# Index scores, one convolution tile and the threshold search of an encoder layer in another order

## Chip, cores and metric

The kernel runs on 1 core of one Trainium2 chip. The metric is the time of one execution on the device in microseconds. Before the change it is 2482.51 us, the median of 3 runs (2481.71 to 2482.91).

## What is computed

One layer of a streaming encoder on 1088 frames (1024 of a prompt, 64 of a sample with 128 cached positions), 1024 features, float32. Cut to the part around the change:

```python
h = x + 0.5 * swiglu(rms(x), ffn1)
u = rms(h); z = u @ w_in              # q, k, v, q_idx, k_idx, w_idx, conv input, gates
q, k, qi, ki = rope(q), rope(k), rope(qi), rope(ki)
s = relu(qi_head @ ki.T)              # 8 index heads
score = sum_head(wi * s)              # per frame and key, keys up to the frame's chunk
keep = top 256 keys of each frame     # (or a quarter of the keys)
attn = softmax(q @ k.T over keep) @ v
c = ca * sigmoid(cb)                  # 512 channels, depthwise causal conv of width 31
conv_out = silu(layernorm(conv(c))) @ conv_w_out
h = h + (g_a * (attn @ attn_w_out) + g_c * conv_out) @ w_out
h = h + 0.5 * swiglu(rms(h), ffn2); y = rms(h)
```

Besides y it returns the new k, v, index keys and the last 30 rows of c.

## The kernel before

Frames lie along the free axis, features on the 128 partitions. Matrix products run as three float32r matmuls (high by high, low by high, high by low half, mm3, L135 to L137). In the middle of the kernel, between the two feed-forward blocks, TensorE makes the projections of u: `uproj(wt, c)` (L551) is one of three column chunks of 364, 362 and 362 frames, 24 matmuls into one PSUM bank. Weights come by DMA in the order of a packed layout and are split into halves by ScalarE (L117) and GpSimd (L118).

The pieces that the change touches:

- `conv_in(t)` (L604): the two projections of convolution tile t (128 of 512 channels), a tanh on ScalarE (L609), a product on VectorE (L618), and the store to DRAM. `conv(t, dve)` (L646) is the depthwise convolution: for tiles 0, 1 and 2 (dve False) ScalarE makes the 30 shifted products (L675) and GpSimd adds them (L676), in two pieces; for tile 3 (dve True) VectorE does 30 multiply-adds (L661) in each of three pieces, 90 in all, with the sum in a PSUM bank.
- `rope` (L564): six operations on VectorE (L574 to L579) on a pair of chunks in PSUM; `rope_pairs` calls it for the index queries and for the queries.
- Index scores (L768 to L788): for seven tiles of frames (sizes L of 384, 512, 640, 768, 896, 1024 keys, and 192 for the sample's 64 frames; numbered 0 to 6 in the code) and eight heads, a pair of matmuls (L778, L779), relu on ScalarE (L780), and a weighted sum into Y on VectorE (L783, L785). 88 pairs in all.
- The threshold search (L803 to L952) finds for each frame the value of its 256th best score, bit by bit: first the upper 15 bits of the scores as int16, then the lower 16. For each bit, `count` counts how many keys lie above a candidate: tiles 5 and 4 (1024 and 896 wide) on ScalarE (L871, settled by L891 and L892), the other five on VectorE (L874, settled by L880, L882, L884). Ahead of it stand first counts and sign flips (L847 to L859), between high and low bits a transition (L920 to L930: one more count of each tile, L925, and a mask, L928), and behind it the bias for the attention (L934 to L952).
- Attention: `soft` makes logits (L1023, L1024) into three banks, VectorE adds the bias and finds the maximum (L1026); then come transposes (L1050) and values. In the background run two of the 16 gate tiles (L965 to L976; 14 stand before), norm(2) of the convolution's LayerNorm (L1112 to L1139), conv_out (L1157) and the merge.

The order on each engine is fixed at build time: a tile framework simulates the program and takes, on each engine, the ready instruction of highest priority. What is written earlier has priority, and `tc.high_priority(THI)` lifts a block: the search stands in such a block, the scores do not. The PSUM of this stage has seven banks for projections and one for conv(3)'s sum, later three for scores, four for projections and that one.

Of the kernel before, what the change touches and what calls it, by code (L numbers as in the profile page):

```python
# [9 lines left out]
F32 = mybir.dt.float32  # L10
# [81 lines left out]
class Kern:  # L92
# [342 lines left out]
    def run(self):  # L435
        tc, nc, a = self.tc, self.nc, self.a
        PS = bass.MemoryType.PSUM
        with ExitStack() as top:
# [260 lines left out]

            conv(0, False)  # L700
            tbs = ExitStack()
            kx = self.pool(tbs, "kidx", 1)
            tb = tables(tbs)
            with ExitStack() as es:
# [12 lines left out]
                wt = self.w()  # L717
                pa = [uproj(wt, c) for c in range(3)]
                wt = self.w()
                for c, (c0, w) in enumerate(CHUNKS):  # L720
                    pb = uproj(wt, c)
                    nc.scalar.activation(wz[:, c0:c0 + w], pa[c][0:8, :], AF.Copy)
                    rope(tb, pa[c], pb, c, d_k, a["ko"])
# [43 lines left out]

            for n, (t0, rows, k0, L, top_) in enumerate(STILES):  # L768
# [70 lines left out]
            for n, (t0, rows, k0, L, top_) in enumerate(STILES):  # L839
# [3 lines left out]
                if n in XT:  # L843
                    nc.gpsimd.memset(lkx[:, c:c + 1], -float(L + 1))
# [17 lines left out]
            def search(bits, dt, res):  # L862

                nc.vector.memset(cand, float(1 << (bits - 1)) - 0.5)
# [12 lines left out]
                def settle(g, b):  # L877

                    half = 0.5 * (1 << b)
# [15 lines left out]
                nc.vector.scalar_tensor_tensor(thx, thr[:, GX], 2.0, lkx, op0=ALU.mult, op1=ALU.add)  # L895
                sb = iter(())
                for b in range(bits - 1, -1, -1):
# [10 lines left out]
                    count(B3[0], b)  # L908
                    next(sa)
                    count(B3[1], b)  # L910
                    next(sa)
                    count(B3[2], b)
                    next(sa)
# [3 lines left out]

            search(15, I16, hib)

            nc.vector.tensor_scalar(cand, hib, 1.0, None, op0=ALU.add)  # L920
            for n in range(NT):
                rows, y0, L = rows_of(n)
                hh = H16[:rows, y0:y0 + L]
                c1 = slice(COL[n], COL[n] + 1)
                nc.vector.tensor_scalar(spare(n), hh, cand[:rows, c1], 0.0,  # L925
                                        op0=ALU.is_ge, op1=ALU.add, accum_out=cnt[:rows, c1])
# [534 lines left out]
```

## Time and profile before

| what | value |
|---|---|
| median of 3 runs | 2482.51 us |
| the profiled execution | 2482.32 us, its span 2480.5 us |
| mean granted clock of TensorE | 0.973 |
| busy: TensorE, VectorE, ScalarE, GpSimd | 2327.5, 1749.5, 1228.2, 1401.5 us |

The profile is of one execution. Engines are PE (TensorE), DVE (VectorE), ACT (ScalarE), POOL (GpSimd) and SP, which issues DMAs. A line such as L661 is a line of the kernel; in the changed kernel the same statement stands two or three lines higher (L659 for L661, L872 for L874, L919 for L920, L927 for L928, L1021 for L1023). [...] In a timeline a row gives the start, the duration, the engine and line, the tiles, and in brackets how long the engine was idle before and on what it waited.

### The profile page before, as it was taken

What the parts mean: (1) busy time and instruction counts of PE and PEld (TensorE: products, weight loads), DVE (VectorE), ACT (ScalarE), POOL (GpSimd) and SP (SyncE); (2) the same over time, 40 slices, a digit from 0 to 9 for tenths busy, and PEclk for the clock granted to TensorE, in tenths of its full rate; (3) what the DMA queues carried; (4) which work ended last, traced back from release to release, by engine and by line L of the source; (5) the groups of instructions that cost most, each with busy time, mean ns of one, the idle gap of its engine ahead of it and who ended that gap; (6) DMA issues with size and microseconds to landing.
All of it is one profiled execution on the core that took longest, in us unless ns stands there. A gap on an engine that the chain in (4) does not pass through costs nothing. (4 is left out here: it accounts for less than half of the span.)

```text
span 2480.5 us, 44631 instructions
## 1 busy us (share of the span) xinstructions
PE 2327.5 (94%) x16762; PEld 2291.3 (92%) x16762; DVE 1749.5 (71%) x4007; ACT 1228.2 (50%) x2423; POOL 1401.5 (56%) x866
## 2 busy tenths in 40 slices
PE   5999999999999999999955999989999999999998
PEld 5999999999999999998954888888999999999998
DVE  7666777766677326699799877548666678676676
ACT  5443444433445457768863556535433445344343
POOL 4555556555556889876512445546555556555554
PEclk9999999999999999999977999999999999999999
DMA  4223223222225333233321444464232232323223
GB/s 161 103 86 103 92 96 122 94 94 98 97 97 175 113 117 100 82 110 119 100 87 38 132 142 140 146 226 130 94 99 90 97 100 82 116 88 118 94 94 113
DMA packets 129977, 271.89 MB, mean 110 GB/s; under 512 B 17888, under 2 KB 77152, under 8 KB 129760
## 3 DMA queue, kind: packets, MB, share of 16 engines
q1 hardware_dynamic: 129760, 269.03, 33.3%
q8 instruction: 132, 2.16, 0.4%
q14 instruction: 85, 0.70, 0.1%
HBM read 230.29 MB, written 38.75 MB: 108 GB/s over the span
## 5 line engine op out<-in xcount | busy, mean ns | idle before, releaser
L118 POOL TENSOR_TENSOR wlo<-raw,whi 128x1024 fp32r<-128x1024 f32 (+1 forms) x187 | 433.5, 2322 | 434.7 <-ACT whi L117 429.5
L135 PE MATMUL ps<-x,wp 128*128 128x272 f32 x1760 | 508.5, 290 | 10.9 <-DVE spare L283 8.9
L135 PE MATMUL ps<-x,whi 128*128 128x272 f32 (+2 forms) x1544 | 485.1, 314 | 23.7 <-ACT sg L974 12.5
L137 PE MATMUL ps<-x,wp 128*128 128x272 f32 x1760 | 506.2, 291 | 1.0 <-DVE wp L152 0.6
L136 PE MATMUL ps<-x,wp 128*128 128x272 f32 x1760 | 506.6, 289 | 0.0
L137 PE MATMUL ps<-x,wlo 128*128 128x272 f32 (+2 forms) x1544 | 482.5, 313 | 0.0
L136 PE MATMUL ps<-x,whi 128*128 128x272 f32 (+2 forms) x1334 | 413.8, 310 | 0.0
L135 PE MATMUL ps<-gh,whi 128*128 128x272 f32 x1408 | 399.5, 289 | 6.8 <-DVE spare L283 5.0
L136 PE MATMUL ps<-gl,whi 128*128 128x272 f32 x1408 | 404.7, 289 | 0.0
L137 PE MATMUL ps<-gh,wlo 128*128 128x272 f32 x1408 | 403.5, 288 | 0.0
L152 POOL TENSOR_TENSOR wlo<-raw,whi 128x1024 fp32r<-128x1024 f32 x88 | 220.3, 2504 | 261.8 <-ACT whi L151 254.3
L135 PEld LDWEIGHTS ps<-x,wp 128*128 128x128 f32 x1760 | 332.8, 189 | 11.9 <-ACT wp L151 11.9
L137 PEld LDWEIGHTS ps<-x,wp 128*128 128x128 f32 x1760 | 330.9, 189 | 2.7 <-DVE wp L152 2.3
L136 PEld LDWEIGHTS ps<-x,wp 128*128 128x128 f32 x1760 | 333.2, 189 | 0.0
L135 PEld LDWEIGHTS ps<-x,whi 128*128 128x128 f32 x1544 | 294.1, 191 | 28.0 <-ACT sg L974 14.4
L152 POOL TENSOR_TENSOR wp<-s,wp 128x512 fp32r<-128x512 f32 x176 | 258.3, 1468 | 94.5 <-ACT wp L151 94.5
L117 ACT ACTIVATE whi<-raw 128x1024 fp32r<-128x1024 f32 (+1 forms) x187 | 190.7, 1020 | 223.9 <-PE ps L136 122.8
L137 PEld LDWEIGHTS ps<-x,wlo 128*128 128x128 f32 x1544 | 294.1, 191 | 0.8
L423 DVE SCALAR_TENSOR_TENSOR h<-ps,h 128x272 f32<-128x272 f32 x384 | 164.2, 437 | 184.9 <-PE ps L137 184.4
L676 POOL TENSOR_TENSOR ac<-ac,pd 128x559 f32<-128x559 f32 x180 | 256.8, 1426 | 49.6 <-ACT pd L675 29.7
L135 PEld LDWEIGHTS ps<-gh,whi 128*128 128x128 f32 x1408 | 262.8, 189 | 8.3 <-DVE spare L283 5.6
L137 PEld LDWEIGHTS ps<-gh,wlo 128*128 128x128 f32 x1408 | 265.7, 189 | 0.0
(228 smaller groups left out, 5039.2 us busy)
## 6 DMA issues: line engine op xcount, KB each, us to landing
raw<-wf SPq DMA_DIRECT2D x334, 512.0 KB, 3.3
raw<-wf SPq DMA_DIRECT2D x32, 384.0 KB, 3.0
d_g<-sg SPq DMA_DIRECT2D x32, 181.0 KB, 1.9
d_h<-h SPq DMA_DIRECT2D x2, 2176.0 KB, 10.6
y<-t SPq DMA_DIRECT2D x32, 136.0 KB, 1.8
raw<-d_q SPq DMA_DIRECT2D x32, 128.0 KB, 2.9
raw<-d_qi SPq DMA_DIRECT2D x24, 128.0 KB, 3.0
d_g<-sg SPq DMA_DIRECT2D x16, 182.0 KB, 2.5
```

The lines of the kernel that those rows point to most:

```text
L117: nc.scalar.activation(hi[:, :n], raw[:, :n], AF.Copy)
L118: self.weng.tensor_tensor(lo[:, :n], raw[:, :n], hi[:, :n], op=ALU.subtract)
L135: t.matmul(out, wh, xh, start=first, stop=False)
L136: t.matmul(out, wh, xl, start=False, stop=False)
L137: t.matmul(out, wl, xh, start=False, stop=last)
L152: (eng or nc.vector).tensor_tensor(lo, x, hi, op=ALU.subtract)
L423: nc.vector.scalar_tensor_tensor(x, p, 0.5, x, op0=ALU.mult, op1=ALU.add)
L676: nc.gpsimd.tensor_tensor(ac, ac, pd, op=ALU.add)
```

## The change

Three things change. The index scores are written in a block of the search's priority, with four banks from the start; projections then have four (seven before) and conv(3)'s sum uses one of the score banks; a rope's two projections are made chunk by chunk in turn. Convolution tile 3 is projected right behind tile 0, and its 90 multiply-adds follow; tiles 1 and 2 are projected ahead of the queries, behind the scores; the packed weights follow this order. In the high pass of the search tile 4 is counted on VectorE, and the transition is made in four groups of tiles, each of which can go on to the low bits alone.

```diff
@@ -591,11 +591,10 @@
                     wa, wb = self.w(), self.w()
-                    pa = [uproj(wa, c) for c in range(3)]
-                    if then and t == 1:
-                        then()
                     for c in range(3):
-                        rope(tb, pa[c], uproj(wb, c), c, dst[:, t * P:(t + 1) * P, :])
+                        rope(tb, uproj(wa, c), uproj(wb, c), c, dst[:, t * P:(t + 1) * P, :])
+                        if then and t == 1 and c == 0:
+                            then()
...
@@ -634,10 +633,9 @@
-            cb_es = ExitStack()
-            cvb = self.pool(cb_es, "cvb", 1, space=PS)
             ps_es = ExitStack()
-            self.ps = self.pool(ps_es, "ps7", 7, space=PS)
+            lgi = self.pool(ps_es, "lgi", 4, space=PS)
+            self.ps = self.pool(ps_es, "ps4", 4, space=PS)
...
-                        ac = cvb.tile([P, 512], F32, name="acc", tag="acc")[:, :w]
+                        ac = lgi.tile([P, 512], F32, name="acc", tag="lgi")[:, :w]
...
+            conv_in(3, ep)
             conv(0, False)
+            conv(3, True)
             tbs = ExitStack()
...
-            ps_es.close()
-
-
-            ps_es = ExitStack()
-            lgi = self.pool(ps_es, "lgi", 3, space=PS)
-            self.ps = self.pool(ps_es, "ps4", 4, space=PS)
...
+            hi = tc.high_priority(THI)
+            hi.__enter__()
             for n, (t0, rows, k0, L, top_) in enumerate(STILES):
                 qt = load_q(xp, d_qi, t0, rows)
...
+            hi.__exit__(None, None, None)
             ix.close()
             conv_in(1, ep)
             conv(1, False)
-
-            rope_pairs(tb, d_q)
-            conv_in(3, ep)
             conv_in(2, ep)
             conv(2, False)
+
+            rope_pairs(tb, d_q)
...
-            XT, A2, B3 = (5, 4), (3, 1), (2, 0, 6)
-            COL = {n: c for c, n in enumerate((*XT, *A2, *B3))}
-            GX, GA, GB = slice(0, 2), slice(2, 4), slice(4, 7)
+            COL = {n: c for c, n in enumerate((5, 4, 3, 1, 2, 0, 6))}
+            GROUPS = {15: ((5,), (4, 3, 1), (2, 0, 6)), 16: ((5, 4), (3, 1), (2, 0, 6))}
...
+                XT, GA, GB = GROUPS[bits]
+                GX = cols(XT)
...
-                    count(A2[0], b)
-                    next(sb, None)
-                    count(A2[1], b)
-                    next(sb, None)
-                    next(sb, None)
+                    for n in GA:
+                        count(n, b)
+                        next(sb, None)
+                    for _ in sb:
+                        pass
...
-            nc.vector.tensor_scalar(cand, hib, 1.0, None, op0=ALU.add)
-            for n in range(NT):
...
-            nc.vector.tensor_tensor(thr, thr, cnt, op=ALU.subtract)
+            for g in ((3, 1), (2, 0, 6), (4,), (5,)):
+                cg = cols(g)
+                nc.vector.tensor_scalar(cand[:, cg], hib[:, cg], 1.0, None, op0=ALU.add)
+                for n in g:
...
+                nc.vector.tensor_tensor(thr[:, cg], thr[:, cg], cnt[:, cg], op=ALU.subtract)
+                nc.vector.memset(cand[:, cg], float(1 << 15) - 0.5)
             search(16, U16, lob)
...
-            conv(3, True)
...
-    conv_cols((0,))
+    conv_cols((0, 3))
...
-    conv_cols((1,))
+    conv_cols((1, 2))
     rope_cols(Q)
-    conv_cols((3, 2))
```

How this moves instructions. On VectorE, between the ropes of the index queries (L574 to L579 read ps, the projections' bank, and write m and ro). Before:

```order
L574 TENSOR_TENSOR m_10720<-ps,cos 128x362
L575 TENSOR_TENSOR ps<-ps,sin 128x362
L576 TENSOR_TENSOR m_10686<-ps,cos 128x362
L577 TENSOR_TENSOR ps<-ps,sin 128x362
L579 TENSOR_TENSOR ro<-m_10686,ps 128x362
L578 TENSOR_TENSOR ro<-m_10685,ps 128x362
L576 TENSOR_TENSOR m_10721<-ps,cos 128x362
L577 TENSOR_TENSOR ps<-ps,sin 128x362
L579 TENSOR_TENSOR ro<-m_10721,ps 128x362
L578 TENSOR_TENSOR ro<-m_10720,ps 128x362
```

With the change; L659 is conv(3)'s multiply-add into acc:

```order
L574 TENSOR_TENSOR m_11011<-ps,cos 128x362
L575 TENSOR_TENSOR ps<-ps,sin 128x362
L659 SCALAR_TENSOR_TENSOR acc<-ci,par,acc 128x372 x4
L576 TENSOR_TENSOR m_11012<-ps,cos 128x362
L577 TENSOR_TENSOR ps<-ps,sin 128x362
L659 SCALAR_TENSOR_TENSOR acc<-ci,par,acc 128x372
L579 TENSOR_TENSOR ro<-m_11012,ps 128x362
L578 TENSOR_TENSOR ro<-m_11011,ps 128x362
L659 SCALAR_TENSOR_TENSOR acc<-ci,par,acc 128x372 x3
L574 TENSOR_TENSOR m_11083<-ps,cos 128x364
L575 TENSOR_TENSOR ps<-ps,sin 128x364
```

The ropes are now each chunk pair's own, and conv(3)'s multiply-adds, which stood in the scores and the search, lie between them.

On TensorE at the start of the attention (lg are logits; L165 and L174 with ones, ident, mu are norm(2)). Before, right behind the last gate:

```order
L165 MATMUL ps<-ones,ls 128x128 x8
L1023 MATMUL lg<-kh_13532,qt 128x512
L1024 MATMUL lg<-kl_13533,qt 128x512
L1023 MATMUL lg<-kh_13532,qt 128x512
L1024 MATMUL lg<-kl_13533,qt 128x512
L1023 MATMUL lg<-kh_13532,qt 128x512
L1024 MATMUL lg<-kl_13533,qt 128x512
L174 MATMUL ps<-ident,mu 128x128 x3
L174 MATMUL ps<-ident,mu 128x8
L165 MATMUL ps<-ones,ls 128x128 x8
L1023 MATMUL lg<-kh_13532,qt 128x512
L1024 MATMUL lg<-kl_13533,qt 128x512
```

With the change, the same norm; ahead of the rows shown are the two last gate tiles, behind the first three logits, and nine more logits:

```order
L1022 MATMUL lg<-kl_13625,qt 128x512
L1021 MATMUL lg<-kh_13624,qt 128x512
L1022 MATMUL lg<-kl_13625,qt 128x512
L165 MATMUL ps<-ones,ls 128x128 x8
L174 MATMUL ps<-ident,mu 128x128 x3
L174 MATMUL ps<-ident,mu 128x8
L1048 MATMUL pt<-ident,pr 128x128 x8
L135 MATMUL pv<-ph,vt 64x256
L1048 MATMUL pt<-ident,pr 128x128 x4
L136 MATMUL pv<-pl,vt 64x256
L137 MATMUL pv<-ph,vt 64x256
```

Norm(2) has moved from around the third logit to behind the twelfth, and the transposes and values of the first attention units follow at once.

On ScalarE at the end of the high pass (hib is its result; L871 and L869 are counts, L675 and L673 the products of a convolution, L974 and L973 gates, L117 weights). Before:

```order
L974 ACTIVATE sg<-ps,hb 128x362
L891 ACTIVATE flag<-cnt,thx 128x1 x2
L892 ACTIVATE hib<-flag,cand 128x1 x2
L974 ACTIVATE sg<-ps,hb 128x364
L974 ACTIVATE sg<-ps,hb 128x362
L117 ACTIVATE whi<-raw 128x1024
L974 ACTIVATE sg<-ps,hb 128x362
L871 ACTIVATE bias,cnt<-H_12869,cand 128x1024
L871 ACTIVATE bias,cnt<-H_12869,cand 128x896
```

With the change:

```order
L973 ACTIVATE sg<-ps,hb 128x364
L890 ACTIVATE flag<-cnt,thx 128x1
L891 ACTIVATE hib<-flag,cand 128x1
L673 ACTIVATE pd<-ci,par 128x559 x2
L973 ACTIVATE sg<-ps,hb 128x362
L673 ACTIVATE pd<-ci,par 128x559 x2
L117 ACTIVATE whi<-raw 128x1024
L973 ACTIVATE sg<-ps,hb 128x362
L673 ACTIVATE pd<-ci,par 128x559 x2
L869 ACTIVATE bias,cnt<-H_12973,cand 128x896
L973 ACTIVATE sg<-ps,hb 128x364
L869 ACTIVATE bias,cnt<-H_12973,cand 128x1024
```

One count per high bit is left on ScalarE. Six products of conv(2) now stand between its last high bit and its first low count, and more follow among the first low bits; before, none came behind the last high bit.

On VectorE the bias of tiles 5 and 4, whose low bits ScalarE counts, comes behind that of the other five, before and with the change.

## Rows read from the trace of the kernel before

**Rows 1.** The page, busy time of each engine, share of the span, instructions.

```profile
PE 2327.5 (94%) x16762; PEld 2291.3 (92%) x16762; DVE 1749.5 (71%) x4007; ACT 1228.2 (50%) x2423; POOL 1401.5 (56%) x866
```

**Rows 2.** Windows: us, then busy us (instructions) per engine, clock, DMA share, GB/s.

```profile
850.00:900.00 50.00, 50.00 (x308) 49.75 (x308) 17.51 (x35) 23.97 (x34) 42.53 (x28) 1.00 0.35 113
1082.00:1111.10 29.10, 29.10 (x177) 29.10 (x177) 27.58 (x42) 13.83 (x21) 19.32 (x28) 1.00 0.36 106
1111.10:1212.40 101.30, 95.44 (x561) 93.96 (x560) 84.29 (x286) 91.79 (x198) 73.79 (x47) 0.98 0.37 116
1225.50:1292.20 66.70, 41.27 (x234) 40.68 (x232) 64.61 (x256) 56.21 (x144) 9.51 (x4) 0.83 0.27 94
```

**Rows 3.** Timeline of PE: start us, us, engine, line, tiles; idle before and releaser.

```profile
1292.33 3.76 PE L165 MATMUL ps<-ones,ls 128*128 128x128 f32 x16 [18.77 <-DVE lob L884]
1326.59 0.80 PE L1023 MATMUL lg<-kh,qt 128*128 128x512 f32 x1 [12.56 <-DVE mb L1026]
1343.86 0.97 PE L135 MATMUL ps<-ch,whi 128*128 128x362 f32 x2 [1.40 <-ACT ch L151]
```

**Rows 4.** Timeline of VectorE from the search's first count to the attention's first use.

```profile
1082.00 0.55 DVE L847 TENSOR_SCALAR_CACHE_REDUCE bias<-Y 128x384 bf16<-128x384 f32 x1
...
1111.16 0.60 DVE L874 TENSOR_SCALAR_CACHE_REDUCE bias<-H,cand 128x384 bf16<-128x384 int16 x1
...
1212.40 1.28 DVE L920 TENSOR_SCALAR cand<-hib 128x7 f32<-128x7 f32 x1 [15.58 <-ACT hib L892]
...
1219.80 5.58 DVE L928 SCALAR_TENSOR_TENSOR H<-H,hib,Y 128x384 uint16<-128x384 int16 x7
...
1225.57 1.00 DVE L874 TENSOR_SCALAR_CACHE_REDUCE bias<-H,cand 128x768 bf16<-128x768 uint16 x1
...
1325.84 0.69 DVE L1026 CUSTOM_DVE_ANT_0 pr<-lg,bias 128x512 f32<-128x512 f32 x1
```

**Rows 5.** Windows of line L661 alone: us, VectorE's busy us (instructions), clock, DMA, GB/s.

```profile
1082.00:1111.10 29.10, 3.50 (x6) 1.00 0.36 106
1111.10:1212.40 101.30, 21.30 (x36) 0.98 0.37 116
```

**Rows 6.** Timeline of PE: first and last pair of score matmuls.

```profile
918.29 0.44 PE L778 MATMUL lgi<-khi,qt 128*128 128x384 f32 x1
...
1081.46 0.25 PE L778 MATMUL lgi<-khi,qt 128*64 128x192 f32 x1
```

**Rows 7.** Timeline of VectorE: one operation of a rope.

```profile
883.75 0.54 DVE L576 TENSOR_TENSOR m<-ps,cos 128x364 f32<-128x364 f32 x1 [7.83 <-PE ps L137]
```

**Rows 8.** Groups by line, 1111 to 1212 us: busy us, mean ns | idle before, releaser.

```profile
L675 ACT ACTIVATE pd<-ci,par 128x559 f32<-128x559 f32 x38 | 28.7, 759 | 0.1
...
L871 ACT ACTIVATE bias<-H,cand 128x1024 bf16<-128x1024 int16 x15 | 17.2, 1145 | 0.0
```

**Rows 9.** Timeline of VectorE: start of one high bit without fill, and of the next.

```profile
1168.60 1.01 DVE L874 TENSOR_SCALAR_CACHE_REDUCE bias<-H,cand 128x768 bf16<-128x768 int16 x1
...
1172.75 1.01 DVE L874 TENSOR_SCALAR_CACHE_REDUCE bias<-H,cand 128x768 bf16<-128x768 int16 x1
```

**Rows 10.** Timeline of VectorE: an 896-wide count of int16 and the next count's start.

```profile
1216.65 1.14 DVE L925 TENSOR_SCALAR_CACHE_REDUCE bias<-H,cand 128x896 bf16<-128x896 int16 x1
...
1217.72 1.27 DVE L925 TENSOR_SCALAR_CACHE_REDUCE bias<-H,cand 128x1024 bf16<-128x1024 int16 x1
```

**Rows 11.** Timeline of VectorE, then of GpSimd: operations side by side.

```profile
1095.74 10.21 DVE L858 TENSOR_SCALAR Y<-Y,sgn 128x384 f32<-128x384 f32 x7
...
1095.75 9.42 POOL L676 TENSOR_TENSOR ac<-ac,pd 128x559 f32<-128x559 f32 x6
...
1211.25 2.39 POOL L118 TENSOR_TENSOR wlo<-raw,whi 128x1024 fp32r<-128x1024 f32 x1 [2.02 <-ACT whi L117]
```

**Rows 12.** Timeline of VectorE: norm(2) among the bias operations.

```profile
1304.23 1.49 DVE L1121 TENSOR_TENSOR lx<-lx,ps 128x392 f32<-128x392 f32 x3
...
1309.19 0.96 DVE L1123 TENSOR_TENSOR ls<-ls 128x784 f32<-128x784 f32 x1
```

More of the change, by code (lines that the diff above doesn't have):

```diff
@@ L715, in run @@
                 nc.sync.dma_start(d_v[:, 8, :], cv)
-                wt = self.w()
-                pa = [uproj(wt, c) for c in range(3)]
-                wt = self.w()
+                wa, wb = self.w(), self.w()
                 for c, (c0, w) in enumerate(CHUNKS):
-                    pb = uproj(wt, c)
-                    nc.scalar.activation(wz[:, c0:c0 + w], pa[c][0:8, :], AF.Copy)
-                    rope(tb, pa[c], pb, c, d_k, a["ko"])
+                    pa = uproj(wa, c)
+                    nc.scalar.activation(wz[:, c0:c0 + w], pa[0:8, :], AF.Copy)
+                    rope(tb, pa, uproj(wb, c), c, d_k, a["ko"])
                 def values_by_row():
@@ L828, in run, with cols @@
             lkx = kp.tile([P, 2], F32, name="lkx")
-            XT, A2, B3 = (5, 4), (3, 1), (2, 0, 6)
-            COL = {n: c for c, n in enumerate((*XT, *A2, *B3))}
-            GX, GA, GB = slice(0, 2), slice(2, 4), slice(4, 7)
+            COL = {n: c for c, n in enumerate((5, 4, 3, 1, 2, 0, 6))}
+            GROUPS = {15: ((5,), (4, 3, 1), (2, 0, 6)), 16: ((5, 4), (3, 1), (2, 0, 6))}
+            def cols(g):
+                return slice(COL[g[0]], COL[g[-1]] + 1)
             nc.gpsimd.memset(cnt, 0.0)
@@ L842, in run @@
                 nc.gpsimd.memset(lmk[:, c:c + 1], float(L - 2 * top_ + 1))
-                if n in XT:
+                if c < 2:
                     nc.gpsimd.memset(lkx[:, c:c + 1], -float(L + 1))
@@ L862, in search @@
             def search(bits, dt, res):
-                nc.vector.memset(cand, float(1 << (bits - 1)) - 0.5)
+                XT, GA, GB = GROUPS[bits]
+                GX = cols(XT)
                 def count(n, b):
@@ L875, in count, with settle @@
                                                 accum_out=cnt[:rows, c:c + 1])
-                def settle(g, b):
+                def settle(t, b):
+                    g = cols(t)
                     half = 0.5 * (1 << b)
@@ L893, in settle_x @@
                                          bias=cand[:, c], scale=-0.5 * (1 << b))
-                nc.vector.scalar_tensor_tensor(thx, thr[:, GX], 2.0, lkx, op0=ALU.mult, op1=ALU.add)
+                nc.vector.scalar_tensor_tensor(thx[:, GX], thr[:, GX], 2.0, lkx[:, GX], op0=ALU.mult, op1=ALU.add)
                 sb = iter(())
@@ L901, in search @@
                         settle_x(n, b)
-                    count(A2[0], b)
-                    next(sb, None)
-                    count(A2[1], b)
-                    next(sb, None)
-                    next(sb, None)
-                    sa = settle(GA, b)
[L908 to L913, printed above, removed]
+                    for n in GA:
[3 more added lines that the diff above has]
+                        pass
+                    sa = settle(GA, b)
+                    for n in GB:
+                        count(n, b)
+                        next(sa)
                     sb = settle(GB, b)
@@ L916, in search @@
                     pass
+            nc.vector.memset(cand, float(1 << 14) - 0.5)
             search(15, I16, hib)
-            nc.vector.tensor_scalar(cand, hib, 1.0, None, op0=ALU.add)
-            for n in range(NT):
[L922 to L926, printed above, removed]
-                lo16 = Y[:rows, y0:y0 + L].bitcast(U16).rearrange("p (n t) -> p n t", t=2)[:, :, 0]
-                nc.vector.scalar_tensor_tensor(hh.bitcast(U16), hh, hib[:rows, c1], lo16,
-                                               op0=ALU.is_equal, op1=ALU.mult)
-            nc.vector.tensor_tensor(thr, thr, cnt, op=ALU.subtract)
+            for g in ((3, 1), (2, 0, 6), (4,), (5,)):
+                cg = cols(g)
+                nc.vector.tensor_scalar(cand[:, cg], hib[:, cg], 1.0, None, op0=ALU.add)
+                for n in g:
+                    rows, y0, L = rows_of(n)
+                    hh = H16[:rows, y0:y0 + L]
+                    c1 = slice(COL[n], COL[n] + 1)
+                    nc.vector.tensor_scalar(spare(n), hh, cand[:rows, c1], 0.0,
+                                            op0=ALU.is_ge, op1=ALU.add, accum_out=cnt[:rows, c1])
+                    lo16 = Y[:rows, y0:y0 + L].bitcast(U16).rearrange("p (n t) -> p n t", t=2)[:, :, 0]
+                    nc.vector.scalar_tensor_tensor(hh.bitcast(U16), hh, hib[:rows, c1], lo16,
+                                                   op0=ALU.is_equal, op1=ALU.mult)
+                nc.vector.tensor_tensor(thr[:, cg], thr[:, cg], cnt[:, cg], op=ALU.subtract)
+                nc.vector.memset(cand[:, cg], float(1 << 15) - 0.5)
             search(16, U16, lob)
-            for g in (GX, GA, GB):
+            for g in map(cols, GROUPS[16]):
                 nc.vector.tensor_copy(mi[:, 0, g], hib[:, g])
@@ L982, in run @@
             ps_es.close()
-            cb_es.close()
             at_es = ExitStack()
```

## Prediction

> **What bounds the kernel now.** I read first where TensorE idles, because the page gives it 94% of the span [rows 1]: only a stage in which it stops can give much back. By the windows it is full around 850 and from 1082 to 1111 us, but busy for only 41.27 of the 66.70 us of the search's low pass, at a clock of 0.83 [rows 2]. The timeline of TensorE then shows the stop itself: after the last gate (1292.33 less the wait, so 1273.6) it sits idle 18.77 us, then 12.56 us before the fourth logit at 1326.59, and the background's first matmul (conv_out) starts at 1343.86 [rows 3]. What it waits for is VectorE: the first L1026 at 1325.84 is the first use of the last stage's bias [rows 4]. From the first count of the search (L847, 1082.00) to there VectorE has work almost without a gap: 27.58 of 29.10 us, 84.29 of 101.30 and 64.61 of 66.70 [rows 2], and the one long gap, 15.58 us before L920, is a wait for ScalarE's high-pass result [rows 4]. So the chain that sets the end is: last score, the search's preparation, 15 high bits, transition, 16 low bits, bias. A microsecond off that chain is a microsecond of TensorE's idle time, as long as TensorE has finished its gates, and about 25 us of such idle time are there to win.
>
> What lies on that chain without belonging to it: 6 of conv(3)'s 90 multiply-adds (L661) in the preparation and 36 in the high pass, 3.50 and 21.30 us [rows 5]. And VectorE is idle at another place: 17.51 us busy of 50 at 850 to 900, while TensorE is full [rows 2].
>
> **The change part by part, against the profiled execution of 2482.32 us (0.19 below the median of the three runs).**
>
> *Scores earlier.* The first pair of score matmuls runs at 918.29 now, the last at 1081.46 [rows 6]. Counted down TensorE's order, 2,190,392 columns stand up to the last score before and 2,172,244 after, though conv_in(3) is now ahead of the first: the 88 pairs are spread over fewer projections. 18,148 columns are 50 matmuls of 363; 177 of them took 29.10 us at full clock [rows 2], 0.164 us each, so 8.2 us earlier. The other way round: the first score stands 59,000 columns later, 26.8 us, so near 945; from it to the last are 344,000 columns now, passed in 163 us, and 267,000 after, 127 us at the same pace, so 1072. I keep the smaller gain of 8.2 us; bounds 0 (VectorE or ScalarE cannot follow the denser scores) and 12. Before the first count GpSimd must also have cleared its sums (L830), which in its order stands behind conv(1): 59 adds at 9.42 / 6 = 1.57 us [rows 11] and nine splits of some 2.4 us are 115 us from about 945, so 1060, in time.
>
> *Conv(3) moved.* Its 90 multiply-adds now stand between the rope operations of k and the index queries (first excerpt of the order), under TensorE's 18 chunks of 24 matmuls, 3.95 us each. A pair of chunks lasts 7.9 us; it needs six rope operations of 0.54 us at most [rows 7], 3.2 us, and the order puts 5 to 9 multiply-adds beside them, at 21.30 / 36 = 0.59 us [rows 5] 3.0 to 5.3 us. That is 6.2 to 8.5 of 7.9 us, so on the whole it is covered by TensorE, with two pairs in the four banks as slack: cost taken as 0. Were the cover gone, 90 of them at 0.59 us, 53 us, would be TensorE's. The step's stores and loads move forward on SP's queue too, where the DMA engines are 35% busy [rows 2]: nothing.
>
> *Preparation.* Without the 6 multiply-adds 3.2 us less (a little under their 3.50 busy us, since neighbours overlap).
>
> *High pass.* Now 1111.16 to 1212.40, 101.2 us [rows 4], with ScalarE counting two tiles beside conv(2)'s products and gates: 15 counts of 1024 take 17.2 us, 38 products 28.7 [rows 8], and with everything else it is busy 91.79 of the 101.30 [rows 2], so ScalarE ends this pass. After: VectorE's bit without filling takes 4.15 us [rows 9], and tile 4 adds its count, 1.07 us from the start of the 896-wide count to the next [rows 10]: 5.22 us, 15 times, 78.3 us. The splits and one query tile that stand in between (k, v) add 5.2 us as they do now. 83.5 us in all: **17.7 us less**. ScalarE, with one count of two gone, has by the same rows room to end earlier than VectorE. Bounds: 78 (the splits fit elsewhere) and 95 us (ScalarE ends the pass again).
>
> *Transition.* Now 13.2 us from L920 to the first low count [rows 4]. The same seven counts and seven masks; new are three more L920, memsets and subtractions on a few columns. One L920 lasts 1.28 us [rows 4], the smaller ones about 0.15. I take +1.8 us, bounds +0.5 and +8. The upper one is a row: the seven L858 took 10.21 us where GpSimd ran six adds of 9.42 us beside them, the seven L928 only 5.58 us with GpSimd idle [rows 4, 11]; and L920, seven columns wide, ended with GpSimd's split that began at 1211.25 [rows 11]. If conv(2)'s adds now reach into the transition, the masks go at L858's pace: +4.6 us, and the four L920 +3. I take the low value because ScalarE's order has only six products left between its last high bit and its first low count, which waits for the transition, so GpSimd should have run dry. [...]
>
> *Low pass.* 16 bits of 4.15 us as now. ScalarE starts its two tiles only after the whole transition and some 17 products now lie in its first six low bits; at 28.7/38 us each [rows 8] that is 13 us more than it has now, in which it ended 8 us ahead. But the order gives the bias of tiles 5 and 4 to VectorE last, about 17 us behind the others: taken as covered, cost 0, bound +8.
>
> *Bias and norm(2).* Between 1292.2 and 1325.84 VectorE also does norm(2): four L1121, of which three take 1.49 us, L1123 with 0.96 [rows 12] and small ones, 3.2 us. In the new order they come behind twelve logits. So 3.2 us less ahead of the first L1026.
>
> Sum up to the first L1026: -8.2 - 3.2 - 17.7 + 1.8 - 3.2 = -30.5, so at about 1295.3.
>
> *Behind it.* The norm's 3.2 us are paid there, and the last gate chunk stands partly behind the fourth logit: 4,612 columns, 2.1 us. Conv_out's first matmul now has 46,000 columns behind the fourth logit instead of 14,000 (second excerpt); these 32,000 columns of attention have to be done anyway, so the background's later start is taken at 0, with +10 as its bound. Together +5.3.
>
> **Sum:** 2482.3 - 30.5 + 5.3 = **2457 us**.
>
> **Rivals.**
>
> *The gain is partly given back at the attention's start* (0.15). For it: TensorE's clock falls when it is idle (0.83 over the low pass [rows 2]), and the background that keeps it busy (from 1343.86 [rows 3]) now waits for the whole norm(2) chain. Against: TensorE's work is the same. At the bound of +10: 2467.
>
> *ScalarE or GpSimd lengthens the search* (0.15): the products in the low pass make tiles 5 and 4 end after the others' bias, or GpSimd's adds slow the transition; each is 8 us: 2465, both 2473.
>
> *Everything comes free* (0.14): the later norm lies in gaps of VectorE, the gate remainder fills a hole, the preparation gains more: the full 33 us, 2449.
>
> *VectorE becomes too full under the projections, and the kernel is slower* (0.07). The multiply-adds queue ahead of the ropes on VectorE, a rope frees its two banks late, and with four banks instead of seven TensorE waits. It decides at 7.9 us of VectorE per pair of chunks, and the estimate above reaches 8.5. For it: the single runs of four or five multiply-adds between two ropes. Against: 32 of 50 us were idle there. If each of the nine pairs costs 4 us, 36 us: 2457 + 36 = 2493. Slower than now from 25 us on, 2.8 us a pair.
>
> *The change does not do what it says* (0.03): scores are limited by ScalarE's relu and the conv products rather than by place, and the search starts when it did; with tile 4 on VectorE the high pass still gains, but if ScalarE also remains the end of it, little is left: 2480.
>
> **How the numbers follow.** The forecast has 0.46. Its own range is 2450 to 2464. For eight in ten I take in the free case (down to 2446) and both that give back (up to 2474); outside remain the slower case, the empty one and some of the tails. A measurement of this kernel can tell about 0.2%, 5 us, from no change. Faster by more than that: 0.46 + 0.15 + 0.15 + 0.14 = 0.90; the empty case is half within: 0.03; slower 0.07.
>
> **What would show it.** Right: the first L847 near 1074, the first high count near 1100, bits of 5.2 us without L661 among them, L920's first group without a long idle time, the first L1026 near 1295, and TensorE's wait before it under 30 us in all. The multiply-adds all lie before 940, and TensorE has no waits for VectorE between 840 and 930. Wrong: idle time of TensorE in that stretch with a rope or a multiply-add as its releaser; a high pass above 90 us; a wait of the bias for ScalarE; or a first L1026 near 1295 with an end that is less than 20 us earlier, which would put the loss behind the search.

## The result and the profile after

The changed kernel takes 2446.04 us (median of 4 runs, 2442.73 to 2447.54) against 2482.11 us for the kernel before in the same session (4 runs): a ratio of 0.9855, 95% interval 0.9838 to 0.9872, so 36 us faster. The profiled execution took 2446.25 us, its span is 2444.3 us, and TensorE's mean granted clock is 0.981 of its full speed.

The page, answering to [rows 1]: the work of each engine is nearly what it was, only the span around it is 36 us shorter.

```profile
PE 2310.1 (95%) x16762; PEld 2277.2 (93%) x16762; DVE 1762.0 (72%) x4046; ACT 1206.3 (49%) x2363; POOL 1403.1 (57%) x866
```

Windows of after, with the columns of [rows 2]: the stretch that now holds conv(3)'s multiply-adds, the search's preparation, the high pass, and the low pass.

```profile
838.00:929.10 91.10, 90.17 (x552) 89.65 (x551) 78.51 (x146) 47.91 (x70) 80.86 (x53) 1.00 0.41 133
...
1065.44:1089.04 23.60, 23.60 (x144) 23.60 (x144) 23.46 (x34) 11.18 (x16) 16.49 (x25) 1.00 0.44 130
1089.04:1172.55 83.51, 77.47 (x466) 76.56 (x464) 81.45 (x274) 65.54 (x125) 67.94 (x43) 1.00 0.37 112
1188.00:1253.50 65.50, 57.78 (x336) 57.34 (x336) 63.23 (x249) 65.41 (x153) 37.74 (x23) 0.94 0.29 96
```

In the first, VectorE goes from 17.51 us of 50 [rows 2] to 78.51 of 91.10, and TensorE still loses less than a microsecond (90.17 of 91.10). In the high pass VectorE (81.45 of 83.51) is the bound and ScalarE (65.54) is not; before, it was ScalarE with 91.79 of 101.30 [rows 2]. In the low pass TensorE has 57.78 us instead of 41.27, and ScalarE is full (65.41 of 65.50): work that stood in the high pass now lies here. TensorE's only wait from 838 to 930 us (total, times, longest) is for neither a rope nor a multiply-add:

```profile
PE ps L729 <- ACT vT L749: 0.9, 1, 0.9
```

VectorE's timeline, answering to [rows 4]: first preparation count, the two halves of the sign step, first high bit, the passage (count limits, then masks), one late cast, and the first use of the bias.

```profile
1065.44 0.55 DVE L844 TENSOR_SCALAR_CACHE_REDUCE bias<-Y 128x384 bf16<-128x384 f32 x1
...
1074.95 4.71 DVE L855 TENSOR_SCALAR Y<-Y,sgn 128x384 f32<-128x384 f32 x3
...
1080.87 5.39 DVE L855 TENSOR_SCALAR Y<-Y,sgn 128x768 f32<-128x768 f32 x4
...
1089.04 0.60 DVE L872 TENSOR_SCALAR_CACHE_REDUCE bias<-H,cand 128x384 bf16<-128x384 int16 x1
...
1172.55 0.21 DVE L919 TENSOR_SCALAR cand<-hib 128x2 f32<-128x2 f32 x2
...
1175.62 2.75 DVE L927 SCALAR_TENSOR_TENSOR H<-H,hib,Y 128x768 uint16<-128x768 int16 x3
...
1183.24 1.73 DVE L927 SCALAR_TENSOR_TENSOR H<-H,hib,Y 128x640 uint16<-128x640 int16 x3
...
1184.97 1.27 DVE L927 SCALAR_TENSOR_TENSOR H<-H,hib,Y 128x1024 uint16<-128x1024 int16 x1
...
1271.14 2.36 DVE L934 CAST mi<-lob 128x2 int32<-128x2 f32 x1
...
1286.28 0.69 DVE L1024 CUSTOM_DVE_ANT_0 pr<-lg,bias 128x512 f32<-128x512 f32 x1 [0.24 <-issue]
```

The first use of the bias comes at 1286.28 instead of 1325.84, 39.6 us earlier; the end of the span is 36.2 us earlier. L919 has no bracket: the 15.58 us in which VectorE waited for ScalarE's last high bit [rows 4] are gone.

TensorE's timeline, answering to [rows 3] and [rows 6]: first and last score, and the idle times.

```profile
939.37 0.34 PE L773 MATMUL lgi<-khi,qt 128*128 128x384 f32 x1
...
1063.51 0.25 PE L774 MATMUL lgi<-kli,qt 128*64 128x192 f32 x1
...
1188.00 0.67 PE L135 MATMUL ps<-x,whi 128*128 128x362 f32 x1 [18.13 <-ACT sg L973]
...
1287.03 0.79 PE L1021 MATMUL lg<-kh,qt 128*128 128x512 f32 x1 [7.24 <-DVE mb L1024]
```

Ahead of the bias TensorE now stops for 7.24 us instead of 18.77 and 12.56 [rows 3]. One stop is new, 18.13 us in the passage, and ScalarE's timeline names its cause: the first low count, of tile 4, waits for that tile's subtraction L929, which VectorE makes only at 1186.18, behind the last of the seven masks (1184.97 and 1.27 us), and the gates that TensorE needs are queued behind that count.

```profile
1186.36 1.04 ACT L869 ACTIVATE bias<-H,cand 128x896 bf16<-128x896 uint16 x1 [21.50 <-DVE srch L929]
```

### The profile page after: what moved, and what is told of

It reads as the page before. It is cut to its first block, busy times and chain, and to the rows that moved or that the text cites. A ratio compares the mean times of both kernels' runs of the same rounds, so it can differ in the third digit from the quotient of the medians.

```text
span 2444.3 us, 44609 instructions
## 1 busy us (share of the span) xinstructions
PE 2310.1 (95%) x16762; PEld 2277.2 (93%) x16762; DVE 1762.0 (72%) x4046; ACT 1206.3 (49%) x2363; POOL 1403.1 (57%) x866
## 3 DMA queue, kind: packets, MB, share of 16 engines
q1 hardware_dynamic: 129760, 269.03, 34.4%
## 5 line engine op out<-in xcount | busy, mean ns | idle before, releaser
L135 PE MATMUL ps<-x,wp 128*128 128x272 f32 x1760 | 508.1, 290 | 11.4 <-DVE spare L283 9.3
L135 PE MATMUL ps<-x,whi 128*128 128x272 f32 (+2 forms) x1544 | 481.9, 312 | 31.3 <-ACT sg L973 21.5
L117 ACT ACTIVATE whi<-raw 128x1024 fp32r<-128x1024 f32 (+1 forms) x187 | 190.5, 1019 | 226.7 <-PE ps L136 110.2
```

Source lines behind the costliest of these rows:

```text
L117: nc.scalar.activation(hi[:, :n], raw[:, :n], AF.Copy)
L135: t.matmul(out, wh, xh, start=first, stop=False)
```

## The experiments

The open question was not whether the sum held but which part of the change pays. **Theory A**: time is what lies on the chain up to the first use of the bias, with the terms of the prediction. Each kernel was timed against the kernel before on the same chip. The table puts them together: ratio to before with its interval; start of the first high count on VectorE; from there to the first use of the bias; the median less that first use; and how long VectorE waited for ScalarE's last high bit. Milestones are of the one profiled execution, which lay up to 5.4 us from its median.

| kernel | median us | ratio | first high count | to first use | median less first use | wait |
|---|---|---|---|---|---|---|
| before | 2482.11 | 1 | 1111.2 | 214.7 | 1156.3 | 15.6 |
| new search alone | 2479.15 | 0.9986 to 1.0011 | 1110.5 | 212.0 | 1156.7 | 0 |
| conv(3) alone | 2490.99 | 1.0036 to 1.0069 | 1122.6 | 213.7 | 1154.7 | 30.0 |
| scores alone | 2445.02 | 0.9844 to 0.9877 | 1057.7 | 231.6 | 1155.7 | 0 |
| scores + new search | 2460.91 | 0.9903 to 0.9946 | 1062.0 | 242.5 | 1156.5 | 0 |
| all but tile 4's move | 2455.64 | 0.9895 to 0.9924 | 1087.8 | 205.5 | 1162.4 | 10.1 |
| **the change** | 2446.04 | 0.9838 to 0.9872 | 1089.0 | 197.2 | 1159.8 | 0 |
| priority alone | 2476.47 | 0.9981 to 1.0002 | 1104.5 | 216.5 | 1155.5 | 14.1 |
| four early banks, old rope loops | 2458.41 | 0.9892 to 0.9939 | 1065.8 | 235.6 | 1157.0 | 1.6 |
| three early banks, new rope loops | 2464.28 | 0.9918 to 0.9963 | 1105.8 | 208.6 | 1150.0 | 11.7 |
| passage in one group | 2455.99 | 0.9887 to 0.9921 | 1092.0 | 195.4 | 1168.6 | 0 |
| ScalarE's tiles first | 2447.44 | 0.9846 to 0.9895 | 1090.6 | 196.7 | 1160.1 | 0 |
| tile 0 on ScalarE too | 2446.73 | 0.9846 to 0.9887 | 1086.1 | 203.1 | 1157.6 | 4.7 |
| scores alone, three tiles on ScalarE | 2465.08 | 0.9930 to 0.9961 | 1057.7 | 250.5 | 1156.9 | 22.6 |

### One part at a time

The new search alone: the search's hunks of the change, on the kernel before.

```diff
-            XT, A2, B3 = (5, 4), (3, 1), (2, 0, 6)
+            GROUPS = {15: ((5,), (4, 3, 1), (2, 0, 6)), 16: ((5, 4), (3, 1), (2, 0, 6))}
...
+            for g in ((3, 1), (2, 0, 6), (4,), (5,)):
```

> The kernel before with only the third part: tile 4 counted by VectorE in the high pass, transition in four groups. Theory A (VectorE's chain from the last score to the first use of the bias sets the end): the high pass then holds 15 bits of 5.22 us, 5.2 us of splits and 35 of conv(3)'s multiply-adds at 0.59 us, 104 us against 101 before, so the first L1026 comes up to 4 us later than 1325.8 and the time is 2481 to 2488. Rival B (ScalarE was the bound of the high pass, and relieving it pays by itself): the 15.58 us of VectorE's wait go, 2466 to 2472.

Measured: 2479.15 us, no gain (the ratio is 0.9999). That is 2 us below theory A's range, and rival B, which gave the wait of 15.58 us back, fell. Conv(3) alone:

```diff
+            conv_in(3, ep)
             conv(0, False)
+            conv(3, True)
...
-            conv_in(3, ep)
             conv_in(2, ep)
...
-            conv(3, True)
```

> The kernel before with only the second part's move of conv_in(3) and conv(3) behind conv_in(0); scores, banks and search as before. Theory A: no multiply-add is left in the search, but the last score stands 42,048 columns later on TensorE, 19 us; the preparation gives 3 to 6 us back, and the high pass is ended by ScalarE's two counts after 90 to 95 us instead of 101. Sum +3 to +8 at the first L1026: 2484 to 2490. Rival C (conv(3)'s 25 us in the search were the cost): 2457 to 2465.

Measured: 2490.99 us, 0.5% slower. Rival C fell; the time lies 1 us above theory A's range, and the high pass is ended by ScalarE after 100.8 us, not after 90 to 95. Windows of each one's high pass, first of the new search alone (up to its last group), then of conv(3) alone:

```profile
1110.50:1216.50 106.00, 98.10 (x571) 96.90 (x569) 104.78 (x332) 71.14 (x135) 71.49 (x45) 0.97 0.36 111
```

```profile
1122.60:1223.40 100.80, 95.26 (x563) 94.38 (x562) 68.66 (x250) 90.06 (x196) 72.84 (x46) 0.98 0.33 103
```

And VectorE's timeline of conv(3) alone at the end of that pass:

```profile
1223.40 0.87 DVE L921 TENSOR_SCALAR cand<-hib 128x7 f32<-128x7 f32 x1 [29.99 <-ACT hib L893]
```

The pass has two engines of nearly equal load (before, 84.29 and 91.79 us of 101.30 [rows 2]). Take a count off ScalarE, and VectorE, with tile 4's counts and conv(3)'s multiply-adds, is busy 104.78 of 106 us. Take the multiply-adds off VectorE, and it waits 30 us for ScalarE, whose 90 us have not changed. Only both together, as in the change, shorten it (83.51 us); the two without the scores part were not run. Conv(3) alone also has its last score 17.1 us later (1098.6), because conv_in(3)'s 144 matmuls now stand ahead of the scores, and its first high count 11.4 us later; that is its loss.

The scores alone: pools, rope loops and priority, with conv(3) and search as before.

```diff
-            cvb = self.pool(cb_es, "cvb", 1, space=PS)
-            self.ps = self.pool(ps_es, "ps7", 7, space=PS)
+            lgi = self.pool(ps_es, "lgi", 4, space=PS)
+            self.ps = self.pool(ps_es, "ps4", 4, space=PS)
```

> The kernel before with only the first part: scores at the search's priority with four banks, ropes chunk by chunk, conv(3)'s sum in a score bank; convolution tiles and search as before. The last score stands 76,888 columns earlier on TensorE, 35 us, but 89 of conv(3)'s 90 multiply-adds now lie in the high pass. Theory A: VectorE ends the high pass after 62.3 + 5.2 + 89 x 0.59 = 120 us instead of 101; with 3 us less ahead of it the first L1026 comes 17 to 20 us earlier: 2463 to 2468. Rival D (the scores' place is the whole gain): 2444 to 2450.

Measured: 2445.02 us. Theory A fell here and rival D's range held: this part alone gives all of the gain. Of theory A's terms the last score came 46 us earlier and not 35, the preparation took 21.2 us instead of 29.2 (8 less, not 3), and the high pass 115.7 us, not 120. The summary row of its score matmuls (shortest, median and longest in ns, first and last start; then the forms) and the window of its high pass:

```profile
L771 PE MATMUL lgi<-khi,qt x88: 247/342/447, 913.6 to 1035.1; 128*128 128x384 f32 x24, 128*128 128x512 f32 x24, 128*128 128x320 f32 x16, 128*128 128x448 f32 x16
```

```profile
1057.70:1173.40 115.70, 110.93 (x660) 110.33 (x659) 114.54 (x340) 96.17 (x205) 81.95 (x52) 0.99 0.38 117
```

The last score comes 46 us earlier than before (1035.1 against 1081.46 [rows 6]). Up to the last score TensorE's order has 76,900 columns fewer than before, 34.7 us at the prediction's 0.164 us per 363 columns. The other 11.7 are not fully explained: 4.7 are there already at the first score (913.6 against 918.29), near 4 come from a denser stretch (121.5 us for some 264,000 columns, 0.460 us per thousand, where before it was 163.2 for 344,400, 0.474), and one execution differs from the next by some microseconds. The search pays 17 us of it back (231.6 against 214.7): all but one of conv(3)'s multiply-adds now fall into the high pass, and VectorE is full there (114.54 of 115.70 us).

### Two parts together

The scores with the new search, conv(3) where it was:

```diff
-            conv_in(3, ep)
             conv(0, False)
-            conv(3, True)
...
+            conv_in(3, ep)
             conv_in(2, ep)
...
+            conv(3, True)
```

(against the changed kernel).

> The scores part and the new search, conv(3) left where it was. 89 of its 90 multiply-adds then lie in the search on VectorE, 0.59 us each, 53 us. Theory J (with conv(3) there, VectorE and not ScalarE ends the high pass, so tile 4's counts on VectorE are pure cost): high pass 83.5 + 45 = 128 us against 115.7 with the scores part alone, first bias use 8 to 14 us later than there, 2452 to 2460 us. Rival K (ScalarE still ends the high pass, and the new search gains by itself): high pass below 112 us, 2434 to 2442 us.

Measured: 2460.91 us, 16 more than with the scores alone, just above the range of theory J, whose mechanism holds: VectorE is busy 133.13 of 133.40 us from the first high count to the last group (next row), and tile 4's counts are pure cost there.

```profile
1062.00:1195.40 133.40, 127.66 (x763) 126.76 (x762) 133.13 (x381) 90.42 (x163) 102.59 (x66) 0.99 0.36 111
```

Everything except tile 4's move:

```diff
-            GROUPS = {15: ((5,), (4, 3, 1), (2, 0, 6)), 16: ((5, 4), (3, 1), (2, 0, 6))}
+            GROUPS = {15: ((5, 4), (3, 1), (2, 0, 6)), 16: ((5, 4), (3, 1), (2, 0, 6))}
```

> The changed kernel with tile 4 back on ScalarE in the high pass, all else as changed. Theory A: ScalarE, with two counts, conv(2)'s products and the gates, ends the high pass after 88 to 95 us instead of 83.5, and VectorE waits for it ahead of the transition: 2450 to 2458. Rival E (without conv(3) beside it the pass is short on either engine, and tile 4's move gives nothing): 2444 to 2448.

Measured: 2455.64 us. Theory A's range held, though ScalarE's pass took 98.2 us, more than the 88 to 95 expected. VectorE waits for ScalarE again:

```profile
1185.97 0.15 DVE L919 TENSOR_SCALAR cand<-hib 128x1 f32<-128x1 f32 x1 [10.06 <-ACT hib L891]
```

So the parts don't add up. The scores alone bring the first use of the bias 36.4 us forward (1325.8 to 1289.4). Conv(3)'s move and the new search then put the first high count 31.3 us back (1057.7 to 1089.0) and return 34.4 in the search (231.6 to 197.2). That exchange is worth nothing that can be measured: 2446.04 against 2445.02.

### Which line of the scores part does it

The priority alone, on the kernel before:

```diff
+            hi = tc.high_priority(THI)
+            hi.__enter__()
             for n, (t0, rows, k0, L, top_) in enumerate(STILES):
...
+            hi.__exit__(None, None, None)
             ix.close()
```

> The kernel before with the scores raised to the search's priority and nothing else. Theory F (the fourth bank, not the priority, gathers the scores): the instructions come in the same order as before, first score near 918, first preparation count near 1082, 2478 to 2484 us. Rival G (the priority does it): first preparation count 15 us or more earlier, 2444 to 2456 us.

Measured: 2476.47 us, ratio 0.9991 with an interval that holds 1. On TensorE the instructions stand in the same order as before through the scores and the search (they first differ in the attention, at 1330 us), and the time is the same. With four banks and the new rope loops, too, the built program has the same order on every engine with and without the priority (it was not run). Next, four early banks with the rope loops of before:

```diff
+            lgi = self.pool(ps_es, "lgi", 4, space=PS)
+            self.ps = self.pool(ps_es, "ps4", 4, space=PS)
...
                     pa = [uproj(wa, c) for c in range(3)]
```

> The kernel before with the pool of four score banks opened before the convolution of tile 0 (which shares it), without the priority, and with the rope loops as they were before. Theory F: 88 score pairs spread over 263,900 columns instead of 344,400, as with the whole scores part: last score near 1035, high pass about 115 us because conv(3) is again under it, 2443 to 2449 us. Rival H (the rope loops by chunk free the banks and so carry the gain): 2470 to 2483 us.

And new loops with early pools, but three score banks, and one bank for the convolution as before:

```diff
-            lgi = self.pool(ps_es, "lgi", 4, space=PS)
+            cvb = self.pool(ps_es, "cvb", 1, space=PS)
+            lgi = self.pool(ps_es, "lgi", 3, space=PS)
```

> As the kernel with the scores part alone, without the priority, but with three score banks and one bank of its own for the convolution, as before; pools opened as early as in the change, ropes by chunk. Theory F: the scores are spread over 349,500 columns again, so the last stands where it did: 2474 to 2484 us. Rival I (the early opening of the pools, so that scores need not wait for the projections' seven banks, brings it): 2444 to 2456 us.

Measured: 2458.41 and 2464.28 us. Neither theory's range holds: each kernel has a part of the gain, 20 and 15 of 36 us. Their score rows, four banks first:

```profile
L772 PE MATMUL lgi<-khi,qt x88: 247/360/468, 924.3 to 1048.7; 128*128 128x384 f32 x24, 128*128 128x512 f32 x24, 128*128 128x320 f32 x16, 128*128 128x448 f32 x16
```

```profile
L770 PE MATMUL lgi<-khi,qt x88: 247/339/398, 919.3 to 1078.6; 128*128 128x384 f32 x24, 128*128 128x512 f32 x24, 128*128 128x320 f32 x16, 128*128 128x448 f32 x16
```

The fourth bank gathers the scores: 124 us from first to last with four, 159 with three, as the 263,900 and 349,500 columns of their orders say. The old rope loops go with a loss of 13 us against the scores alone: windows of 800 to 900 us, first with the old loops, then of the scores alone with the new ones, show TensorE idle for 9.66 against 4.85 us of 100. About half of the 10.7 us by which the first score is later lies there. With the old loops TensorE waits for ropes (last row below), with the new ones it doesn't. So 3.8 us are shown to be waits for a bank that a rope still holds; the rest was not traced.

```profile
800.00:850.00 50.00, 45.21 (x258) 44.64 (x257) 15.69 (x35) 25.59 (x41) 40.41 (x32) 0.93 0.34 110
850.00:900.00 50.00, 45.13 (x275) 44.20 (x275) 17.51 (x35) 25.46 (x34) 44.09 (x30) 1.00 0.33 101
```

```profile
800.00:850.00 50.00, 46.82 (x276) 46.52 (x275) 14.79 (x33) 25.41 (x38) 40.55 (x31) 0.97 0.39 122
850.00:900.00 50.00, 48.33 (x300) 47.82 (x299) 14.96 (x31) 25.19 (x36) 44.25 (x29) 1.00 0.31 92
```

TensorE's waits for a rope with the old loops, 780 to 1060 us (total, times, longest):

```profile
PE ps L135 <- DVE ro L579: 3.8, 3, 1.5
```

The three-bank kernel gains another way: its scores end where they did, but conv(3)'s multiply-adds begin at 1021.5 and are done at 1146.1 (before, 1028.3 and 1163.6), and the high pass takes 93.5 us instead of 101.2. Which line moves them was not separated.

### The passage, and attempts to beat both

```diff
-            for g in ((3, 1), (2, 0, 6), (4,), (5,)):
+            for g in ((5, 4, 3, 1, 2, 0, 6),):
```

> The change with the passage from high to low bits in one group again. Theory A (only what lies on VectorE's chain up to the bias counts, and the passage has the same seven counts and masks either way): three L918 and a few short ones less, 1 to 2 us earlier at the first use of the bias, 2443 to 2448 us. Rival N (passing group by group is a gain of its own, VectorE starting low counts while ScalarE finishes): the passage takes 5 us or more longer, 2450 to 2458 us.

Measured: 2455.99 us, in rival N's range, but not by its mechanism. The search is 1.8 us shorter (195.4 against 197.2), as theory A had it. The loss lies behind the first use of the bias (1168.6 against 1159.8). With this edit the order of the attention's instructions on TensorE comes out different too (from 1425.7 us on), and TensorE waits longer for one of its merges; rows of its waits from 1280 to 1620 us (total, times, longest), first of this kernel, then of the change:

```profile
PE ps L135 <- DVE ga L1184: 21.0, 6, 13.1
```

```profile
PE ps L135 <- DVE ga L1184: 12.2, 5, 5.2
```

ScalarE's two tiles first:

```diff
-            for g in ((3, 1), (2, 0, 6), (4,), (5,)):
+            for g in ((5,), (4,), (3, 1), (2, 0, 6)):
```

> The change with ScalarE's tiles 5 and 4 first in the passage. ScalarE's wait of 21.5 us ahead of its first low count falls to about 10, and TensorE's idle time behind it from 18.1 to about 8. Theory A (TensorE has finished its gates before the bias comes, so its idle time in the search costs nothing): first use of the bias within 2 us of 1286, 2442 to 2448 us. Rival M (the idle time has become the bound): the 10 us come back in the end, 2433 to 2438 us.

Measured: 2447.44 us (2442.02 to 2451.72). That proves little: ScalarE still waits 21.7 us, now for VectorE's last L930, and TensorE's wait is 16.1 us, so the wait that was to shrink did not.

```profile
ACT bias L869 <- DVE cand L930: 21.7, 1, 21.7
```

```profile
PE ps L135 <- ACT sg L973: 19.8, 3, 16.1
```

Tile 0 on ScalarE too, first in the changed kernel, then with the scores alone:

```diff
-            GROUPS = {15: ((5,), (4, 3, 1), (2, 0, 6)), 16: ((5, 4), (3, 1), (2, 0, 6))}
+            GROUPS = {15: ((0, 5), (4, 3, 1), (2, 6)), 16: ((5, 4), (3, 1), (2, 6, 0))}
...
-            for g in ((3, 1), (2, 0, 6), (4,), (5,)):
+            for g in ((5,), (4,), (3, 1), (2, 6, 0)):
```

> The change with tile 0 counted on ScalarE in the high pass too, and ScalarE's tiles first in the passage. Theory A: VectorE ends the high pass, and a bit becomes 0.53 us shorter: high pass 83.5 - 8 = 75.5 us, first use of the bias near 1278, 2435 to 2441 us. Rival L (ScalarE, 65.5 us busy of the 83.5, gets 15 counts and 30 small steps of about 1.3 us together, 85 us, and ends the pass): no gain or a loss, 2445 to 2452 us.

```diff
+            GROUPS = {15: ((0, 5, 4), (3, 1), (2, 6)), 16: ((5, 4), (3, 1), (2, 6, 0))}
```

> The scores part alone with conv(3) left in the search, and tile 0 beside tiles 5 and 4 on ScalarE in the high pass, ScalarE's tiles first in the passage. Theory J (with conv(3) there VectorE is the bound, 114.5 us busy of 115.7, ScalarE 96.2): tile 0's 15 counts go from VectorE, 8 us: high pass near 108 us, 2435 to 2442 us. Rival L (ScalarE gets about 20 us and ends the pass): 116 us or more, 2445 to 2452 us.

Measured: 2446.73 and 2465.08 us. Rival L in both; the second even passes its range. VectorE gets through its bits faster (the passage begins 78.6 us after the first high count instead of 83.5, and 88.6 instead of 115.7, there with 22 of conv(3)'s multiply-adds still to come) and then stands still for 4.66 and 22.61 us; its timelines, in the same order:

```profile
1177.62 0.45 DVE L921 TENSOR_SCALAR cand<-hib 128x3 f32<-128x3 f32 x1 [4.66 <-ACT hib L891]
```

```profile
1190.64 0.87 DVE L920 TENSOR_SCALAR cand<-hib 128x3 f32<-128x3 f32 x1 [22.61 <-ACT hib L890]
```

The busy share had misled me: ScalarE was busy only 96.17 of 115.7 us with the scores alone, yet with the third tile it is busy 117.53 of 132.90 us, so its idle time falls from 19.5 to 15.4 us only and the pass ends 17 us later. I put that down to its bits being a chain (count, compare, next limit) between products and gates that come in their own order; no run separates this. No version tried beats both kernels; the scores alone, with far fewer edits, equals the change.

## Why the prediction was right, and where not

The time, 2446.04 us, lies 0.04 us inside the low edge of the range 2446 to 2474 and outside the forecast's own 2450 to 2464; that it falls inside is luck. The gain of 36 us is larger than the 25 forecast. The frame held. Behind the first use of the bias thirteen of the fourteen kernels have 1150 to 1163 us left, whatever happened ahead of it (in the fourteenth TensorE waits longer for a merge), so what is gained before that point is gained in the run, to within those few microseconds.

Step by step, from the two profiled executions (its own sum: 30.5 us up to that point, 39.6 measured):

- *Scores earlier*: 8.2 forecast, 16.6 measured (1082.00 to 1065.44), above the upper bound of 12. This is **the term that was mis-sized**. Some of it is scatter: in the means, the first preparation count starts 12.7 us earlier in the five kernels with the order of the change (1065.4 to 1068.5) than in the three with the order of before (before, new search alone, priority alone: 1076.9 to 1082.0), which is still more than the columns give. The prediction had counted columns at one pace, and TensorE got through them faster in two places. The first score comes at 939.37, where the prediction's columns put it near 945; why the stretch ahead of it is denser was not traced. From there 267,200 columns take 123.9 us, 0.464 us per thousand, where before it was 163.2 for 344,400, 0.474; that is 2.6 us. More important, it took this as one term. It is the difference of two large ones, 46 us earlier by the scores part (1081.5 to 1035.1) and 28 later by conv(3) (to 1063.5), and a reader of the sum would have kept the wrong part of the change.
- *Conv(3) moved*: cost 0 forecast. True of its 90 multiply-adds: they lie from 838.0 to 929.1, and in that stretch TensorE waits for no rope and no multiply-add. Not true of the part as a whole: conv_in(3)'s matmuls ahead of the scores were in the columns, hidden in the net 8.2.
- *Preparation*: 3.2 forecast, 5.6 measured. VectorE's busy time falls by 4.1 us (27.58 [rows 2] to 23.46), 3.5 of it the multiply-adds, and its idle time by 1.4.
- *High pass*: 17.7 forecast, 83.5 us; measured 83.51. The bits are 5.22 us as forecast (two counts of one tile start at 1165.16 and 1170.38); that the whole agrees to a hundredth is chance. Its reasoning, VectorE takes over from ScalarE as the end of the pass, is what the two kernels with one part alone show.
- *Passage and low pass*: 1.8 more forecast, 0.7 measured (80.27 to 81.0). The low value was right for the reason given: between 1169 and 1190 us GpSimd does nothing (its next add, at 1190.32, comes after 21.07 us), the seven masks take 2.75 + 1.73 + 1.27 us against 5.58 [rows 4], and the four L919 take 0.16 us at most each. ScalarE's products in the low bits were covered. GpSimd is idle because ScalarE stands 21.5 us at its first low count, as the prediction had it; what it had not named is that TensorE stands 18.13 us behind that count. The sum had not seen an OR of two columns in this stretch that took 2.22 us (last section); without it the stretch would be shorter than before.
- *Bias and norm(2)*: 3.2 forecast, 0.4 measured (33.17 to 32.73). The norm's operations are gone from the stretch (on TensorE norm(2) stands behind the fifteenth logit, not the twelfth), but a cast of two columns takes 2.36 us where before two of these casts took 0.3 together. GpSimd's timeline shows a weight split of 3.53 us beside it, begun at 1269.94; the cast ends with it, at 1273.50 against 1273.47. Before, GpSimd did nothing in this stretch (0.00 us busy of 33.17).

```profile
1269.94 3.53 POOL L118 TENSOR_TENSOR wlo<-raw,whi 128x1024 fp32r<-128x1024 f32 x1 [16.34 <-ACT whi L117]
```

- *Behind it*: 5.3 more forecast, 3.4 measured (span less first use, 1154.7 to 1158.0), within what single executions differ by.

The rivals: VectorE did not become too full under the projections (78.51 of 91.10 us). The rival that the change does not do what it says, the scores being limited by ScalarE's relu rather than by place, failed, and the bank runs show the opposite of it: place decides, for with three banks the scores end where they did (1078.6 against 1081.5). Of the two that give something back, the attention's start cost 3.4 us and not 15, and the passage and low pass became 0.7 us longer and not 8 or 16 beyond the sum's 1.8. "Everything comes free" at 2449 came nearest in time, but mostly not for its reasons: of these only the preparation gained more (5.6 us).

## What to carry to other kernels

Run the parts of a change alone before crediting any of them: here one part carries the whole gain. The two others are worthless or harmful alone; added to it, the new search costs 16 us, conv(3)'s move (with the passage in groups, but tile 4 left on ScalarE) 11, and both whole together nothing. In the high pass, which two engines shared almost evenly, taking work off one of them alone gained nothing (ratios 0.9999 and 1.0053), and ScalarE's idle share, 19.5 of 115.7 us with the scores alone, did not show that one more chain of dependent steps fits into it: with the third tile the pass ended 17 us later. How far ahead a producer's results can be put (here one more bank) moved a whole block of work in the order, the scores standing within 124 us instead of 159, which a priority alone did not (ratio 0.9991).

## What was not expected of the hardware

Two VectorE instructions of two columns lasted until a GpSimd instruction beside them ended: the cast above, 2.36 us, and in the profile after also an OR of 128x2 at 1251.40, 2.22 us, beside a split from 1251.26 to 1253.60. Elsewhere in that profile the same lines take 0.16 us at this width (L934 at 1251.20, L936 at 1273.53). Not every narrow instruction did: L881, which reads one operand (srch) from a PSUM bank, began beside the same split and took 0.16 us, and none of its 62 took longer. Their rows, VectorE then GpSimd:

```profile
1251.33 0.16 DVE L881 TENSOR_TENSOR flag<-cnt,srch 128x3 f32<-128x3 f32 x1
1251.40 2.22 DVE L936 TENSOR_TENSOR mth<-mi 128x2 int32<-128x2 int32 x1
```

```profile
1251.26 2.34 POOL L118 TENSOR_TENSOR wlo<-raw,whi 128x1024 fp32r<-128x1024 f32 x1 [8.58 <-ACT whi L117]
```

What the rows show is 4.58 us for two steps that elsewhere take 0.32 together; why these two last so long and L881 does not, no run separates. So in this kernel a chain of narrow steps is to be costed by what GpSimd may run beside it, as these rows show it, and not by the width of the steps alone.
